# Low parts of the mixers' weights: an accumulating DMA in place of a subtraction

## The chip, the cores and the metric

The kernel runs on one core of one Trainium2 chip. The metric is the device time of one execution in microseconds (us). Five engines matter here: TensorE (PE in the profile; its weight loads are PEld) multiplies, VectorE (DVE), ScalarE (ACT) and GpSimd (POOL) do elementwise work, and SyncE (SP) issues most of the transfers. Each engine works through its own instruction list in order and waits at an instruction until what that needs is there.

## What is computed

The reference is two layers over 512 positions of 1024 features, all in float32. Each layer has a mixer and a feed-forward part:

```
h = rms_norm(x, attn_norm[l])
q_a, k_c, ..., c_q, c_kv, k_r, u = split(h @ w_in[l])
o_a = nsa_attention(q_a, k_c, ...)            # 6 heads: compressed, selected and window branch
o_b = mla_attention(c_q, c_kv, k_r, ..., w_uq, w_uk, w_uv)   # 6 heads
o_c = s5_ssm(u, ..., w_glu, b_glu)            # state-space groups
mix = concatenate([rms_norm(o_a), rms_norm(o_b), rms_norm(o_c)])
x = x + mix @ w_out[l]
x = x + conv_ffn(rms_norm(x, ffn_norm[l]), ffn_w_up[l], ..., ffn_w_down[l])
```

After the second layer comes a last rms_norm.

## The kernel before

Activations are kept transposed: features on the 128 partitions, the 512 positions along the row, so x is eight tiles of 128x512. Float32 accuracy comes from splitting: an operand is held as a high part (rounded to the format that TensorE takes at full rate, fp32r) and a low part (the operand less its high part), and `mm3` (lines 239 to 242) makes each product with three matmuls: high by high (line 240), weight high by activation low (241), weight low by activation high (242).

Every weight comes through `wload` (lines 232 to 237). SyncE loads 128 x n raw floats from HBM into one of 3 buffers `raw` (line 234). `split` then has ScalarE copy them, rounding, into the high half of one of 4 buffers `wt` (line 226), and GpSimd or VectorE subtract the high half from raw into the low half (line 227). Both sets of buffers are rings: a raw buffer is free for the next load when the subtraction has read it, a wt buffer when the last matmul that uses it is done. Which engine subtracts is set by `eng` in CFG for the weights named there (G is GpSimd, V VectorE); a `wload` without a name uses VectorE.

A layer goes through these weights in turn: 32 tiles of `win` (the input projection, 128x512), then among the attention heads one `wuv` (128x384), six `wuq` (128x384), three `wuk` (128x128), one `wglu` (128x512), and `wout1` (lines 1102 to 1112: for each of eight output tiles one of 128x256 and one of 128x384), then eight of 128x384 in the loop of lines 1150 to 1158, here called the last weights of w_out, whose product is scaled (line 1156), added to x (line 1157) and split for the feed-forward part. That part loads 88 tiles of `wup` (GpSimd subtracts) and 48 tiles of `wdn` (VectorE) a layer.

At the start ScalarE and VectorE split x (lines 229, 230) and square it (lines 286, 288), GpSimd adds the squares (line 294), TensorE sums them over partitions (line 253), and VectorE makes the reciprocal root from that (lines 256 to 268). The products of win begin before that root is known; it scales their results when they are taken out (line 689).

The program is written as tasks in an order by hand (PLAN0, PLAN1). Then a scheduler puts each engine's instructions in order by its own model of their durations; a change of what an instruction costs in that model can move others on every engine.

Of the kernel before, what the change touches and what calls it, by code (L numbers as in the profile page):

```python
# [13 lines left out]
AF = mybir.ActivationFunctionType  # L14
OP = mybir.AluOpType
# [6 lines left out]
D = 1024  # L22
# [108 lines left out]
def _pre(names):  # L131
    return tuple((n, -1, None) for n in names.split())


# The order in which each layer's mixer is issued. An entry is (task, step of the head pipeline, instruction of the
# tensor engine that it stays behind as (stage, unit) or None); step -1 comes before the first head.
PLAN0 = _pre('vc kc q2 cmp0 q0 tab krg q1 rope cmp1 ks kw pa0 vs sp0 gates pa1 ca sp1 pa2 sp2 pa3 sp3 ') + (
# [11 lines left out]
    ("w0", 17, (3, 13)), ("w1", 18, (0, 15)), ("w2", 19, (1, 16)), ("w3", 19, (3, 15)), ("w4", 20, (3, 16)))  # L149
CFG = dict(plan=(PLAN0, PLAN1), F=dict(main=15, aux=10, side=12), R=dict(main=16, side=3, q=3, pr=2), nraw=3, nw=4, hp=50,  # L150
           order=(2, 1, 3, 0), rings=dict(), tabs=2, lead=(0, 0, 3, 4), units=('NNNNNNMMMMMM', 'NNNNNNMMMMMM'), rest=((-7, -1, -1, -5, -7, -1, -1, -1), (-1, -1, -3, -1, -1, -1, -1, -1)),
           eng=dict(wo="G", mix="G", klo="G", csub="G", gel="G", win="G", wup="G", wdn="V", wo2="V", q="G", xadd="V"))


@with_exitstack
def tile_trunk(ctx, tc, xT_in, pos, cst_in, small_in, win, wuq, wuk, wuv, wglu, wout, wup, wdn,
# [6 lines left out]
    pp = ctx.enter_context(tc.tile_pool(name="pp", bufs=1, space=PSUM))  # L163

    def eng(n):
        return dict(V=V, G=G)[cfg["eng"][n]]

    def mk(shape, name, dt=F32):
        return cp.tile(shape, dt, name=name)
# [62 lines left out]
    def wload(src, n, E=None, w=None):  # L232
        raw = nxt("raw", raws)[:, :n]
        SY.dma_start(raw, src)
        w = w or nxt("w", wts)
        split(raw, w[:, 0, :n], w[:, 1, :n], E=E)
        return w

    def mm3(p, w, o, x, start, stop, n=128):
# [415 lines left out]
    for l in range(L):  # L655
# [114 lines left out]
                split(p[r0:r0 + 64], KF[b][r0:r0 + 64, 0], KF[b][r0:r0 + 64, 1])  # L770

        def mla_v():
            uv = wload(wuv[l], 384)
            mv.extend(R.get() for _ in range(3))
            for i in range(4):
                p = ps("mm")
                a0, a1 = ckv[0][:, 0, i * 128:(i + 1) * 128], ckv[0][:, 1, i * 128:(i + 1) * 128]
                PE.matmul(p[:, :384], lhsT=a0, rhs=uv[:, 0, :384], start=True, stop=False)
                PE.matmul(p[:, :384], lhsT=a0, rhs=uv[:, 1, :384], start=False, stop=False)
                PE.matmul(p[:, :384], lhsT=a1, rhs=uv[:, 0, :384], start=False, stop=True)  # L780
                for m in range(3):
                    v = mvv(m)[:, i]
                    split(shp(p[:, m * 128:(m + 1) * 128], 2, 64), v[:, :, 0, :], v[:, :, 1, :])
# [104 lines left out]

        def glu():
            area("side")  # L890
            gw = wload(wglu[l], 512)
            hb = sml(2)
            V.tensor_scalar(hb, S(l, "bglu"), 0.5, None, op0=OP.mult)
            oc = []
            for m in range(2):
                p = ps("x")
                for k in range(2):
                    mm3(p, gw, k * 256 + m * 128, zps[k], k == 0, k == 1)
                t = F.get()
                A.activation(t, p, AF.Tanh, bias=hb[:, m:m + 1], scale=0.5)  # L900
                V.scalar_tensor_tensor(t, t, 1.0, zs[m], op0=OP.add, op1=OP.mult)
                oc.append(t)
            F.free(*zs)
            R.free(*zps)
            mixc.extend(oc)
            area("main")
# [18 lines left out]
        def mla_unit(m, b):  # L925
            st = {}

            def proj_q():
                if b == 0:
                    p = ps("kq")  # L930
                    mm3(p, wload(wuk[l, :, m * 128:(m + 1) * 128], 128), 0, ckv[0], True, True)
                    for x in range(2):
                        r0 = 64 * x
                        split(p[r0:r0 + 64], KF[x][r0:r0 + 64, 0], KF[x][r0:r0 + 64, 1])
                uq = wload(wuq[l, m, :, b * 384:(b + 1) * 384], 384)
                p = ps("kq")
                for k in range(3):
                    mm3(p, uq, k * 128, cq[k], k == 0, k == 2)
# [211 lines left out]
        for c in range(8):  # L1150
            w = wload(wout[l, c, :, wcol[late]:wcol[late] + 384], 384, eng("wo2"))
            p = ps("mm")
# [170 lines left out]
```

## Time and profile before

| what | value |
|---|---|
| time, median of 3 runs (lowest to highest) | 1371.96 us (1371.95 to 1377.19) |
| span of the profiled execution | 1372.3 us |
| PE busy | 1302.4 us, 95% |
| DVE busy | 856.5 us, 62% |
| POOL busy | 724.4 us, 53% |
| ACT busy | 638.8 us, 47% |
| moved by DMA | 140.14 MB, 102 GB/s |

The profile is of one execution. Its span of 1372.3 us runs from its first recorded event to its last; no other time of that execution is recorded, so the span stands for it, and it is 0.3 us above the median of the timed runs.

In the span the first layer's mixer runs to about 322 us, its last weights of w_out to 351 us, its feed-forward part to 715 us; the second mixer follows to 976 us, its last weights of w_out to 1009 us, its feed-forward part to 1343 us, and the final norm ends it. An engine's row in a timeline gives the start, the duration, the line and the tiles, and in brackets the idle time of the engine before it with what ended that. A matmul's recorded duration overlaps that of its neighbours, so a rate is taken from the number of matmuls in a stretch.

### The profile page before, as it was taken

What the parts mean: (1) busy time and instruction counts of PE and PEld (TensorE: products, weight loads), DVE (VectorE), ACT (ScalarE), POOL (GpSimd) and SP (SyncE); (2) the same over time, 40 slices, a digit from 0 to 9 for tenths busy, and PEclk for the clock granted to TensorE, in tenths of its full rate; (3) what the DMA queues carried; (4) which work ended last, traced back from release to release, by engine and by line L of the source; (5) the groups of instructions that cost most, each with busy time, mean ns of one, the idle gap of its engine ahead of it and who ended that gap; (6) DMA issues with size and microseconds to landing.
All of it is one profiled execution on the core that took longest, in us unless ns stands there. A gap on an engine that the chain in (4) does not pass through costs nothing.

```text
span 1372.3 us, 19205 instructions
## 1 busy us (share of the span) xinstructions
PE 1302.4 (95%) x6414; PEld 1079.2 (79%) x6414; DVE 856.5 (62%) x1733; ACT 638.8 (47%) x1322; POOL 724.4 (53%) x722
## 2 busy tenths in 40 slices
PE   7888989998998999999999999999999999999997
PEld 5676777786876888888888887877878888888886
DVE  6988889858695334643466488986764433442455
ACT  4334667754443233423443356886453323332344
POOL 7485546654759155545437665556376315612532
PEclk9989999999999999999999999999999999999998
DMA  6243622212333333443353433121223333333332
GB/s 224 83 131 99 182 85 66 68 62 64 98 99 113 111 95 100 117 124 95 112 173 112 149 124 106 59 60 43 83 85 106 95 100 99 94 92 106 95 94 83
DMA packets 91556, 140.14 MB, mean 102 GB/s; under 512 B 15553, under 2 KB 36545, under 8 KB 91457
## 3 DMA queue, kind: packets, MB, share of 16 engines
q1 hardware_dynamic: 90176, 134.72, 32.2%
q0 software_dynamic: 1280, 4.20, 1.0%
q8 instruction: 50, 0.82, 0.3%
q14 instruction: 50, 0.40, 0.1%
HBM read 125.01 MB, written 15.96 MB: 103 GB/s over the span
## 4 chain that ended last, share of the span: by engine, by line
PE 72%; DVE 19%; issue 3%; POOL 2%; ACT 2%; DMA 2%; SPq 0%; DVEq 0%; POOLq 0%; ACTq 0%
PE bank L240 21%; PE bank L241 20%; PE bank L242 20%; DVE r L227 3%; PE bank L519 2%; PE bank L548 2%; DVE f L520 2%; PE bank L544 2%; DVE r L230 1%; DVE f L304 1%; DVE f L1157 1%; PE bank L271 1%; PE bank L816 1%; PE bank L253 1%; POOL wt L227 1%
## 5 line engine op out<-in xcount | busy, mean ns | idle before, releaser
L240 PE MATMUL bank<-r,wt 128*128 128x512 f32 x1466 | 580.9, 397 | 15.2 <-ACT wt L226 7.3
L241 PE MATMUL bank<-r,wt 128*128 128x512 f32 x1466 | 577.0, 394 | 4.4 <-DVE r L230 3.6
L242 PE MATMUL bank<-r,wt 128*128 128x512 f32 x1466 | 573.4, 394 | 5.1 <-POOL wt L227 5.1
L227 POOL TENSOR_TENSOR wt<-raw,wt 128x512 fp32r<-128x512 f32 (+2 forms) x272 | 355.0, 1309 | 300.1 <-ACT wt L226 291.0
L226 ACT CAST wt<-raw 128x512 fp32r<-128x512 f32 (+2 forms) x398 | 231.0, 584 | 332.5 <-PE bank L241 189.6
L240 PEld LDWEIGHTS bank<-r,wt 128*128 128x128 f32 x1466 | 278.2, 190 | 77.2 <-ACT wt L226 8.9
L242 PEld LDWEIGHTS bank<-r,wt 128*128 128x128 f32 x1466 | 278.0, 190 | 66.1 <-POOL wt L227 8.5
L241 PEld LDWEIGHTS bank<-r,wt 128*128 128x128 f32 x1466 | 278.4, 190 | 62.8 <-DVE r L230 6.5
L227 DVE TENSOR_TENSOR wt<-raw,wt 128x512 fp32r<-128x512 f32 (+3 forms) x126 | 88.9, 709 | 51.7 <-ACT wt L226 51.3
L294 POOL TENSOR_TENSOR f<-f,f 128x512 f32<-128x512 f32 (+1 forms) x53 | 68.0, 1284 | 99.9 <-ACT f L286 98.4
L532 POOL TENSOR_SCALAR f<-f,sml 128x128 f32<-128x128 f32 (+3 forms) x144 | 79.3, 569 | 52.2 <-DVE sml L530 18.0
L227 DVE TENSOR_TENSOR r<-bank,r 128x256 fp32r<-128x256 f32 (+4 forms) x196 | 90.2, 476 | 24.2 <-ACT r L226 23.0
L1182 DVE TENSOR_TENSOR f<-bank,f 128x512 f32<-128x512 f32 x44 | 30.3, 690 | 112.6 <-PE bank L242 103.1
L1188 POOL TENSOR_TENSOR f<-f,f 128x512 f32<-128x512 f32 x44 | 58.0, 1320 | 74.6 <-ACT f L1187 74.6
L523 ACT ACTIVATE f<-f,sml 128x384 f32<-128x384 f32 (+3 forms) x144 | 80.6, 560 | 32.5 <-DVE sml L520 31.6
L226 ACT CAST r<-bank 128x256 fp32r<-128x256 f32 (+4 forms) x196 | 79.0, 417 | 31.8 <-PE bank L544 15.7
L548 PE MATMUL bank<-r,r 128*128 128x512 f32 (+3 forms) x288 | 82.1, 353 | 10.4 <-DVE r L227 7.5
L519 PE MATMUL bank<-r,r 128*128 128x128 f32 (+3 forms) x336 | 79.3, 339 | 9.8 <-DVE sml L520 9.5
L226 ACT CAST r<-f 128x512 fp32r<-128x512 f32 (+1 forms) x76 | 46.9, 620 | 80.5 <-DVE f L1189 65.7
L520 DVE CUSTOM_DVE_ANT_0 f<-bank,cst 128x384 f32<-128x384 f32 (+3 forms) x144 | 67.8, 481 | 12.7 <-PE bank L519 11.6
L1189 DVE TENSOR_TENSOR f<-bank,f 128x512 f32<-128x512 f32 x44 | 30.4, 690 | 72.7 <-POOL f L1188 68.9
L1217 DVE TENSOR_TENSOR f<-bank,f 128x512 f32<-128x512 f32 x48 | 32.7, 688 | 65.6 <-PE bank L242 65.5
(225 smaller groups left out, 1549.9 us busy)
## 6 DMA issues: line engine op xcount, KB each, us to landing
raw<-in_wup_dram SPq DMA_DIRECT2D x176, 256.0 KB
raw<-in_wdn_dram SPq DMA_DIRECT2D x72, 256.0 KB
raw<-in_win_dram SPq DMA_DIRECT2D x64, 256.0 KB
f<-pd SPq DMA_DIRECT2D x32, 256.0 KB
raw<-in_wout_dram SPq DMA_DIRECT2D x32, 192.0 KB
f<-in_xT_dram SPq DMA_DIRECT2D x16, 256.0 KB
f<-in_w_dram SPq DMA_DIRECT2D x16, 256.0 KB
pd<-f SPq DMA_DIRECT2D x16, 256.0 KB
```

Of the source, the lines that this page charges most:

```text
L226: A.copy(hi, src)
L227: (E or V).tensor_tensor(lo, src, f32(hi), op=OP.subtract)
L240: PE.matmul(p, lhsT=w[:, 0, o:o + n], rhs=x[:, 0], start=start, stop=False)
L241: PE.matmul(p, lhsT=w[:, 0, o:o + n], rhs=x[:, 1], start=False, stop=False)
L242: PE.matmul(p, lhsT=w[:, 1, o:o + n], rhs=x[:, 0], start=False, stop=stop)
L294: G.tensor_tensor(a, a, q, op=OP.add)
L519: PE.matmul(p[:, :w], lhsT=q[:, i * 128:w], rhs=k[:, :w], start=n == 0, stop=n == len(passes) - 1)
L520: V.tensor_tensor_reduce(out=sm[i], in0=p[:, :w], in1=C("mask")[:, 512 - w:], op0=OP.add, op1=OP.min, scale=1.0, scalar=3.0e38, accum_out= ...
L523: A.activation(sm[i], sm[i], AF.Exp, bias=mx[:, i:i + 1], scale=-1.0, accum_out=su[:, i:i + 1])
L532: G.tensor_scalar(sm[i], sm[i], rs[:, i:i + 1], 1.0, op0=OP.mult, op1=OP.mult)
L548: PE.matmul(o[:, j * 128:], lhsT=v[j], rhs=pr[:, x, :w], start=first and j == 0 and x == 0, stop=last and j == 3 and x == 1)
L1188: G.tensor_tensor(t, t, r_f, op=OP.mult)
```

## The change

A third way to make a low part, "D", is added to `wload`. ScalarE still copies raw into the high half. Then ScalarE writes the negated high half into the low half, and GpSimd issues a DMA that reads the same weights from HBM a second time and adds them to what stands in the low half. The weights named wo, win and wo2 in `eng` go this way, and so do wuv, wglu, wuk and wuq; wup (GpSimd) and wdn (VectorE) stay as they are.

```diff
-           eng=dict(wo="G", mix="G", klo="G", csub="G", gel="G", win="G", wup="G", wdn="V", wo2="V", q="G", xadd="V"))
+           eng=dict(wo="D", mix="G", klo="G", csub="G", gel="G", win="D", wup="G", wdn="V", wo2="D", q="G", xadd="V"))
...
-        return dict(V=V, G=G)[cfg["eng"][n]]
+        return dict(V=V, G=G, D="D")[cfg["eng"][n]]
...
-        split(raw, w[:, 0, :n], w[:, 1, :n], E=E)
+        if E == "D":
+            A.copy(w[:, 0, :n], raw)
+            A.activation(w[:, 1, :n], w[:, 0, :n], AF.Identity, scale=-1.0)
+            G.dma_start(w[:, 1, :n], src, accum_op=OP.add)
+        else:
+            split(raw, w[:, 0, :n], w[:, 1, :n], E=E)
...
-            uv = wload(wuv[l], 384)
+            uv = wload(wuv[l], 384, "D")
...
-            gw = wload(wglu[l], 512)
+            gw = wload(wglu[l], 512, "D")
...
-                    mm3(p, wload(wuk[l, :, m * 128:(m + 1) * 128], 128), 0, ckv[0], True, True)
+                    mm3(p, wload(wuk[l, :, m * 128:(m + 1) * 128], 128, "D"), 0, ckv[0], True, True)
...
-                uq = wload(wuq[l, m, :, b * 384:(b + 1) * 384], 384)
+                uq = wload(wuq[l, m, :, b * 384:(b + 1) * 384], 384, "D")
```

In the changed kernel a line past the edit has a number five higher (240 is 245, 253 is 258, 294 is 299, 1156 is 1161), and the DMA is line 239.

Over both layers 134 weights are made in the new way: 64 of 128x512 (win), 32 of wout1 (16 of 128x256, 16 of 128x384), 16 last weights of w_out (128x384), and 22 others. That is 96 subtractions less on GpSimd, 38 less on VectorE, 134 instructions more on ScalarE and 134 DMAs more issued by GpSimd. TensorE has the same matmuls, in another order.

GpSimd's list near the program's start, before the change (line 227 is the subtraction of a weight, 294 the adding of squares; f8 and f9 gather the squares, wt0 to wt3 are the weights' buffers):

```order
L227 TENSOR_TENSOR wt0_127<-raw0_124,wt0_127 128x512
L227 TENSOR_TENSOR wt1_128<-raw1_125,wt1_128 128x512
L294 TENSOR_TENSOR f8_71<-f8_71,f10_73 128x512
L294 TENSOR_TENSOR f9_72<-f9_72,f11_74 128x512
L227 TENSOR_TENSOR wt2_129<-raw2_126,wt2_129 128x512
L992 MEMSET f3_66 128x64 x2
L294 TENSOR_TENSOR f8_71<-f8_71,f12_75 128x512
L294 TENSOR_TENSOR f9_72<-f9_72,f13_76 128x512
L992 MEMSET f4_67 128x64 x2
L623 TENSOR_SCALAR smt_160<-smt_160 128x2 x2
L227 TENSOR_TENSOR wt3_130<-raw0_124,wt3_130 128x512
L294 TENSOR_TENSOR f8_71<-f8_71,f14_77 128x512
```

And the same place after it (line 239 is the accumulating DMA, 299 the adding of squares):

```order
L239 DMA wt0_127<-in_win_dram 128x512
L239 DMA wt1_128<-in_win_dram 128x512
L299 ISA
L299 TENSOR_TENSOR f9_72<-f9_72,f11_74 128x512
L299 TENSOR_TENSOR f8_71<-f8_71,f10_73 128x512
L997 MEMSET f3_66 128x64 x2
L299 TENSOR_TENSOR f9_72<-f9_72,f13_76 128x512
L299 TENSOR_TENSOR f8_71<-f8_71,f12_75 128x512
L997 MEMSET f4_67 128x64 x2
L239 DMA wt2_129<-in_win_dram 128x512
L299 TENSOR_TENSOR f9_72<-f9_72,f15_78 128x512
L628 TENSOR_SCALAR smt_160<-smt_160 128x2 x2
```

Where four subtractions stood among the additions there are now the DMAs, and the DMAs of the third and fourth weight stand later among them.

TensorE's list at the place where it sums the squares over partitions (line 253), before the change:

```order
L242 MATMUL bank1_152<-r6_106,wt3_130 128x512
L240 MATMUL bank1_152<-r7_107,wt3_130 128x512
L241 MATMUL bank1_152<-r7_107,wt3_130 128x512
L242 MATMUL bank1_152<-r7_107,wt3_130 128x512
L253 MATMUL bank4_155<-ones_162,f8_71 128x1 x4
L253 MATMUL bank4_155<-ones_162,f9_72 128x1 x4
L242 MATMUL bank2_153<-r0_100,wt0_127 128x512
```

And after it, where that sum is line 258:

```order
L245 MATMUL bank1_152<-r4_104,wt3_130 128x512
L246 MATMUL bank1_152<-r4_104,wt3_130 128x512
L245 MATMUL bank2_153<-r0_100,wt0_127 128x512
L246 MATMUL bank2_153<-r0_100,wt0_127 128x512
L258 MATMUL bank4_155<-ones_162,f8_71 128x1 x4
L258 MATMUL bank4_155<-ones_162,f9_72 128x1 x4
L247 MATMUL bank0_151<-r4_104,wt2_129 128x512
```

The sum stood behind the last product of the first four weights; now it stands some 20 rows earlier, among products of wt0 and wt3, and most products with wt2 and wt3 come behind it.

VectorE's list at the last weights of w_out of the first layer, before the change (1156 scales a product, 1157 adds it to x, 230 makes the low part of x for the feed-forward part, 227 subtracts for a weight):

```order
L1156 TENSOR_TENSOR f13_76<-bank1_152,f16_79 128x512
L230 SCALAR_TENSOR_TENSOR r13_113<-f35_98,smt_160,r13_113 128x512
L1157 TENSOR_TENSOR f27_90<-f27_90,f13_76 128x512
L230 SCALAR_TENSOR_TENSOR r3_103<-f25_88,smt_160,r3_103 128x512
L227 TENSOR_TENSOR wt1_128<-raw2_126,wt1_128 128x384
L1156 TENSOR_TENSOR f1_64<-bank0_151,f16_79 128x512
L227 TENSOR_TENSOR wt2_129<-raw0_124,wt2_129 128x384
L230 SCALAR_TENSOR_TENSOR r4_104<-f27_90,smt_160,r4_104 128x512
L1157 TENSOR_TENSOR f30_93<-f30_93,f1_64 128x512
```

And after it (1161 and 1162 are the former 1156 and 1157):

```order
L1161 TENSOR_TENSOR f13_76<-bank1_152,f16_79 128x512
L230 SCALAR_TENSOR_TENSOR r13_113<-f35_98,smt_160,r13_113 128x512
L1162 TENSOR_TENSOR f27_90<-f27_90,f13_76 128x512
L230 SCALAR_TENSOR_TENSOR r3_103<-f25_88,smt_160,r3_103 128x512
L1161 TENSOR_TENSOR f1_64<-bank0_151,f16_79 128x512
L1162 TENSOR_TENSOR f30_93<-f30_93,f1_64 128x512
L230 SCALAR_TENSOR_TENSOR r4_104<-f27_90,smt_160,r4_104 128x512
```

The weights' subtractions are gone from the list; the rest is the same work in nearly the same order.

## Rows read from the trace of the kernel before

**Rows 1.** page: busy times of the engines; shares of the chain that ended last

```profile
PE 1302.4 (95%) x6414; PEld 1079.2 (79%) x6414; DVE 856.5 (62%) x1733; ACT 638.8 (47%) x1322; POOL 724.4 (53%) x722
...
PE 72%; DVE 19%; issue 3%; POOL 2%; ACT 2%; DMA 2%; SPq 0%; DVEq 0%; POOLq 0%; ACTq 0%
```

**Rows 2.** windows: length, busy (instructions) PE, PEld, DVE, ACT, POOL; clock, DMA share, GB/s

```profile
0.00:50.00 50.00, 39.48 (x178) 31.34 (x179) 37.16 (x66) 21.04 (x35) 33.06 (x34) 0.97 0.52 174
...
50.00:100.00 50.00, 40.46 (x186) 33.66 (x185) 46.23 (x86) 18.81 (x33) 35.73 (x41) 0.90 0.41 123
...
200.00:250.00 50.00, 48.06 (x274) 40.21 (x274) 42.76 (x131) 40.41 (x107) 28.71 (x38) 0.97 0.23 71
...
1050.00:1100.00 50.00, 50.00 (x222) 41.42 (x221) 23.29 (x29) 18.19 (x30) 18.62 (x15) 1.00 0.33 93
```

**Rows 3.** TensorE's waits: waiter <- releaser, us in total, times, longest

```profile
PE bank L519 <- DVE sml L520: 9.5, 8, 3.1
...
PE bank L242 <- POOL wt L227: 5.1, 7, 2.3
...
PE bank L829 <- DVE f L828: 3.6, 1, 3.6
...
PE bank L240 <- DVE f L1156: 3.0, 2, 1.6
...
PE bank L816 <- DVE bd L834: 2.3, 1, 2.3
```

**Rows 4.** timeline, GpSimd: start, duration, work [wait before it]

```profile
21.49 2.99 POOL L294 TENSOR_TENSOR f<-f,f 128x512 f32<-128x512 f32 x2
```

**Rows 5.** busy time and DMA load, 4 to 20 us

```profile
4.00:20.00 16.00, 10.67 (x30) 7.14 (x31) 13.08 (x11) 10.59 (x19) 12.89 (x14) 0.97 0.97 341
```

**Rows 6.** timeline, VectorE, 27 to 39 us

```profile
27.72 0.16 DVE L256 TENSOR_SCALAR sml<-bank 128x4 f32<-128x4 f32 x1 [5.64 <-PE bank L253]
...
36.28 0.69 DVE L304 SCALAR_TENSOR_TENSOR f<-f,f 128x512 f32<-128x512 f32 x1
...
37.22 1.78 DVE L304 SCALAR_TENSOR_TENSOR f<-f,f 128x512 f32<-128x512 f32 x1
```

**Rows 7.** GpSimd's subtractions of line 227, 24 to 112 us

```profile
24.00:112.00 88.00, 34.96 (x25) 0.94 0.37 112
```

**Rows 8.** granted clock after two waits of TensorE

```profile
67.00:70.00 3.00, 2.92 (x8) 2.44 (x9) 2.94 (x5) 2.19 (x3) 1.91 (x1) 0.50 0.01 3
...
118.00:125.00 7.00, 6.00 (x15) 4.62 (x16) 5.95 (x18) 2.01 (x7) 2.21 (x2) 0.51 0.32 90
```

**Rows 9.** timeline, VectorE, the last weights of w_out, first layer

```profile
330.21 1.03 DVE L227 TENSOR_TENSOR wt<-raw,wt 128x384 fp32r<-128x384 f32 x1
```

**Rows 10.** groups of one form: busy time, mean ns

```profile
L1187 ACT ACTIVATE f<-f 128x512 f32<-128x512 f32 x44 | 27.8, 632 | 66.9 <-DVE f L1185 66.9
...
L227 POOL TENSOR_TENSOR wt<-raw,wt 128x512 fp32r<-128x512 f32 x240 | 326.3, 1364 | 275.8 <-ACT wt L226 270.9 <-PE bank L242 1.9 <-PE bank L241 1.4
...
L227 DVE TENSOR_TENSOR wt<-raw,wt 128x384 fp32r<-128x384 f32 x38 | 24.1, 633 | 7.4 <-ACT wt L226 7.4
...
L683 POOL DMA_DIRECT2D f<-ud x4 | 2.4, 601 | 0.4 <-DMA ud<-f 0.4
```

**Rows 11.** GpSimd's own DMAs: size, median us from issue to landing

```profile
ud<-f POOLq DMA_DIRECT2D x4, 256.0 KB, 4.1
...
f<-ud POOLq DMA_DIRECT2D x4, 256.0 KB, 3.4
```

**Rows 12.** timeline, first weight of the second layer: cast, first low part

```profile
715.01 0.61 ACT L226 CAST wt<-raw 128x512 fp32r<-128x512 f32 x1
...
717.69 0.50 PE L242 MATMUL bank<-r,wt 128*128 128x512 f32 x1
```

**Rows 13.** timeline, a weight of w_out: cast, first low part

```profile
306.04 0.51 ACT L226 CAST wt<-raw 128x384 fp32r<-128x384 f32 x1 [0.93 <-PE bank L241]
...
309.73 0.39 PE L242 MATMUL bank<-r,wt 128*128 128x512 f32 x1
```

## Prediction

> **What bounds the kernel now.** I read the page first, then windows of 50 us, then TensorE's waits, then the timeline where those waits are long. TensorE is busy 1302.4 of 1372.3 us, and the chain that ended last runs 72% on it and 19% on VectorE [rows 1]: some 70 us are all that better supply can win, beside what matmuls lose at half clock. The windows say where: in the feed-forward part TensorE is busy 50.00 of 50 us, but 39.48 and 40.46 in the first two windows, where VectorE works 46.23 of 50 and GpSimd 35.73 [rows 2]. The idle time is the mixers', in the first 100 us above all. The feed-forward's weights are not touched, so I expect nothing there.
>
> TensorE's waits name VectorE first: 9.5 us for scores, 3.6 and 2.3 for the compressed branch (lines 829 and 816), 3.0 for the sums into x (1156). GpSimd's weight subtraction itself stands there with only 5.1 us in seven waits [rows 3]. So taking the subtraction away wins little directly; what it can win is VectorE's time, which GpSimd stretches: the same instruction of line 304 takes 0.69 us alone and 1.78 us at 37.22, under a subtraction [rows 6].
>
> **The change, term by term.** Low part alone, GpSimd: a 128x512 subtraction takes 1.36 us (240 such rows), and issuing a DMA of the same 256 KB from GpSimd 0.60 [rows 10]. So GpSimd is relieved by about 0.76 us a weight. VectorE loses 38 subtractions of 0.63 us, 24 us in all [rows 10]. ScalarE gains 134 negations; the nearest row, a 128x512 activation in place, takes 0.63 us [rows 10]: some 80 us on an engine that is never more than 40.41 busy of 50 in the windows shown [rows 2].
>
> *Latency of a low part.* Before, it lands a subtraction (1.36 us) behind the cast. After: negation 0.63, then issue to landing of an accumulating DMA, which the trace does not have. GpSimd's plain DMAs of 256 KB into and out of SBUF land after 3.4 and 4.1 us [rows 11]. Below 3.4 nothing speaks for it; above, an accumulation that reads its target first as a pass of its own would be up to twice that, 6.8. I take 4.5, near the rows. So a low part comes about 5.1 us behind the cast instead of 1.4.
>
> *What hides it.* A full load of win feeds 12 matmuls, at 50.00 us for 222 matmuls [rows 2] 2.7 us of TensorE. With four buffers, three others cover 8.1 us while one is refilled; less cast and negation (1.25) that leaves 6.9 us for the landing, so 4.5 is hidden in the steady state. The last weights of w_out feed nine matmuls: 6.1 us of cover, less two passes of 0.5, leaves 5.1; hidden, barely. It is not hidden where a weight is needed soon after its cast. The second layer's first weight is cast until 715.62 and its low part used at 717.69 [rows 12]: 2.07 us there, 5.1 needed, 3.0 lost. A weight of w_out is cast until 306.55 and used at 309.73 [rows 13]: 3.18 there, 4.8 needed, 1.6 lost. Sum **+5** for the late low parts; 0 if the scheduler's new order moves these uses back, +15 if the landing takes 6.8 (2.3 more at each of some four such places).
>
> *The start.* The subtractions between the additions of squares go, four of them: 4 x 0.76 = 3.0 us of GpSimd. The last squares are added until 24.48 [rows 4], and VectorE then sits idle 5.64 us until 27.72 for the sum that TensorE makes of them [rows 6]. TensorE's new list has that sum some 20 rows earlier, so up to 3 us come off the time at which VectorE's long list begins; with TensorE's own rows ahead of the sum out of the way, 4. Against it: from 4 to 20 us the transfers already keep the DMA engines 0.97 busy at 341 GB/s [rows 5], and four more reads of 0.26 MB are 1.05 MB, 3.1 us more of queue ahead of x's last tiles; the low part of the first weight is also wanted four rows of TensorE behind its first use. Bounds -4 to +3; I take **-1**.
>
> *VectorE, 24 to 112 us.* GpSimd makes 25 subtractions of line 227 there, 34.96 us; three of them are of activations and stay [rows 7]. Each of the other 22 stretched VectorE by 0 to 1.09 us (row 37.22 less row 36.28 [rows 6]), 0 to 24 us. VectorE is the engine that TensorE waits for here. What can come back is those waits (3.6 + 2.3, and 3.1 as the longest for scores [rows 3]) and what follows them: after the wait of 3.6 the granted clock is 0.50 from 67 to 70 us, after that of 3.1 it is 0.51 from 118 to 125 [rows 8], that is 1.2 and not 2.4 GHz, so 1.5 and 3.4 us are lost. Together 13.9. The relief is of the size of the waits, but GpSimd still adds, multiplies and casts beside VectorE; I take two thirds, **-9** (0 to -14).
>
> *Last weights of w_out, both layers.* VectorE loses 16 of its 38 subtractions, 10 us, one of which took 1.03 us at 330.21 [rows 9]. TensorE waits there 3.0 us for line 1156 in two waits [rows 3]. The wait at the head of the stage depends on the reciprocal root as well, so I take **-2** (-4 to 0).
>
> *ScalarE.* With about eight loads in 200 to 250 us and 0.5 us each it is 44 instead of 40.41 busy of 50 [rows 2], and its exponentials stand behind the negations. The cover is TensorE's own work, 48.06 of 50; if it fails, a wait of a negation's length in a few heads: 0 to +3, I take **0**. In the ring, a negation waits for the last low-part matmul of the buffer's former use, one matmul later than the cast did.
>
> Sum: 5 - 1 - 9 - 2 + 0 = **-7**. The profiled span is 1372.3 us, 0.3 above the median of the runs, so 1372.0 - 7 = **1365 us**.
>
> **A rule that speaks against it.** GpSimd's four DMA issues of line 683 took 601 ns in the mean [rows 10], with no sign of a block. The Trainium skill, "SBUF — State Buffer", section "Who interferes with whom", says that a DMA issued by GpSimd can be starved while VectorE holds the port pair the two share, as copies, casts and tensor_scalar operations in their two-port modes do. By it each landing would stretch by some tenths of a microsecond while VectorE is as busy as at 50 to 100 us: the sum would stand near -5 instead of -7, by an estimate of 0.4 us at a handful of short places. Four rows decide little; no run here shows an accumulating DMA.
>
> **Rivals.**
>
> *The landing is slow (slower).* If an accumulating DMA lands only after 8 us, the ring of four no longer hides it. Place: the projections and the last weights of w_out. Price: at win 8 - 6.9 = 1.1 us a turn, a quarter per load, 64 loads: 18, of which other work of TensorE hides half, 9; at the last weights of w_out (8 - 5.1)/4 x 16 = 12; the four short places 3.5 us worse each, 14 on top of the 5. Less the relief of 12: 9 + 12 + 19 - 12 = +28, **1400 us**. At 6.5 us it is 0 + 6 + 13 - 12 = +7, from where it decides. For it: nothing in the trace accumulates, and the early DMA engines are full [rows 5]. Against: 3.4 and 4.1 us for the plain ones [rows 11], and a DMA share of 0.23 to 0.41 after the first 50 us [rows 2].
>
> *The relief is eaten (no change).* The chain through VectorE from the start to 112 us keeps its length because x comes 3 us later and GpSimd's remaining work stretches VectorE as before: -9 becomes -3, the start +1, w_out -1, late parts +5: +2, **1374 us**. For it: 19% of the chain on VectorE is mostly its own work.
>
> *More comes back.* The first two windows hold 20 us of idle TensorE [rows 2]. If VectorE is early enough from 28 us on, all of its 13.9 us go, the start gives 4, w_out 4, and the low parts cost 2: -20, **1352 us**.
>
> **Chances.** The forecast 0.42, spread from 1357 to 1373; the slow landing 0.20, from 1378 to 1410; the relief eaten 0.20, from 1368 to 1380; more comes back 0.18, from 1343 to 1357. The range that leaves no more than 2 in 10 out is **1347 to 1390**; the forecast's own is 1357 to 1373. A difference under 0.5%, 6.9 us, is about what a measurement here can't tell from none. Faster by more, under 1365.1: all of the last case and 0.26 of the forecast's 0.42, 0.44. Slower by more, over 1378.8: the slow landing and little of the eaten relief, 0.23. Within: the rest, 0.33.
>
> **What would show it.** Right: in the changed profile VectorE's rows of line 304 near 37 us are 0.7 us and not 1.78; VectorE's idle time before the reciprocal root ends by 25 us; the waits of 3.6 and 3.1 us and the half clock behind them shrink; new waits of TensorE name the weight's DMA, in total some 5 us, the largest near the second layer's first weight; the landing stands at 4 to 5 us. Wrong: landings of 6.5 us and more with waits of the low-part matmul spread over the projections; a start in which x arrives later than 20 us and nothing is won by 112; a feed-forward part that changes its length; or waits for ScalarE among the heads of several microseconds.

## The result and the profile after

The changed kernel takes 1394.95 us (median of 4 runs, 1393.77 to 1404.0), the kernel before beside it 1374.58 us (1371.95 to 1377.43). The ratio is 1.0159, with a 95% interval from 1.0123 to 1.0196: about 20 us slower, where 1365 us, 7 us faster, was forecast, and outside the range that ended at 1390. The profiled execution has a span of 1392.0 us, 19.7 us more than before.

The page of the changed kernel, its busy times, its DMA queues and its chain [rows 1]:

```profile
PE 1305.2 (94%) x6414; PEld 1081.1 (78%) x6414; DVE 813.8 (58%) x1695; ACT 703.9 (51%) x1456; POOL 711.1 (51%) x760
...
q1 hardware_dynamic: 90176, 134.72, 32.5%
q0 software_dynamic: 20576, 33.04, 14.3%
...
PE 67%; DVE 10%; DMA 5%; POOL 5%; issue 4%; ACT 3%; SPq 0%; DVEq 0%; POOLq 0%; ACTq 0%
```

VectorE has become 43 us lighter, as meant, and its share of the chain has fallen from 19% to 10%; but DMA stands there with 5% in place of 2%, and POOL too. TensorE's own work is the same, so the 20 us are idle time and time at half clock. GpSimd has lost only 13 us: the issues eat most of what the subtractions gave back.

TensorE's waits after [rows 3] (waiter, releaser, us in total, times, longest):

```profile
PE bank L247 <- DMA wt<-in_win_dram: 18.8, 11, 6.5
PE bank L553 <- DVE r L227: 11.2, 16, 1.5
PE bank L245 <- ACT wt L237: 8.4, 3, 6.0
PE bank L245 <- DVE f L1161: 8.4, 3, 3.8
```

The waits for VectorE at lines 829 and 816 that headed the forecast (3.6 and 2.3) are gone from the list. In their place are the low parts' DMA, and the sums into x (line 1161, the former 1156), which went from 3.0 to 8.4 us.

Where the difference arises is read by setting the two timelines beside each other at landmarks that both kernels have: VectorE's first instruction of a reciprocal root (line 256, later 261), and the last time that it takes a product of win out in the first layer (line 689, later 694). "d" is the start in a kernel less the start before, in us, from the profiled execution of each. Behind "after" the columns are the runs e1, e2, e5, e3, e8, e9, e11 and e15 of the next section. A column is one execution, and not always a typical one: that of e1 took 2.9 us and that of e11 5.0 us more than its run's median, those of e5, e8 and e15 some 2 us less.

| landmark (us before) | after | win only | w_out only | last of w_out only | small only | no DMA, negated only | negated, then added | after + wup by VectorE | same, quarter |
|---|---|---|---|---|---|---|---|---|---|
| first root, 27.7 | -3.0 | -1.8 | 0.0 | +0.3 | -0.6 | -0.7 | +0.9 | -1.7 | -3.5 |
| last of win, 169.3 | -6.4 | -4.0 | +0.3 | -0.1 | +2.6 | -20.2 | +6.0 | -4.7 | -12.2 |
| ahead of the last of w_out, 318.4 | +3.8 | +1.9 | -0.6 | -2.3 | +6.1 | -9.5 | +9.1 | +5.4 | -7.1 |
| behind it, 352.7 | +8.7 | +3.4 | +4.5 | +2.5 | +6.1 | -11.4 | +8.3 | +3.7 | -8.8 |
| second layer's first root, 725.9 | +15.0 | +9.2 | +7.2 | +6.1 | +6.2 | -11.5 | +11.1 | +9.9 | -5.8 |
| ahead of its last of w_out, 973.6 | +14.7 | +9.7 | +7.1 | +5.1 | +5.1 | -9.5 | +14.8 | +10.0 | -6.6 |
| behind it, 1009.6 | +19.7 | +9.7 | +10.4 | +10.3 | +5.1 | -8.9 | +16.8 | +11.3 | -6.4 |
| last root, 1362.7 | +19.9 | +9.6 | +10.7 | +10.4 | +6.6 | -8.7 | +17.0 | +11.5 | -6.2 |

The other columns belong to the experiments. The column "after" alone says: the first projections do win (3.0 us at the first root, 6.4 at the last of win), then the heads of the first layer lose 10.2, the last weights of w_out 4.9 and 5.0, and the second layer's start about 5. In the projections and heads of the second layer, some 250 us, nothing changes.

**The start and the landing.** The first root, and the wait for the first low part, in the changed kernel's timelines [rows 6]:

```profile
24.71 0.16 DVE L261 TENSOR_SCALAR sml<-bank 128x4 f32<-128x4 f32 x1 [2.58 <-PE bank L258]
```

```profile
14.56 0.80 PE L247 MATMUL bank<-r,wt 128*128 128x512 f32 x1 [6.52 <-DMA wt<-in_win_dram]
```

The root comes 3.0 us earlier although TensorE stands for 6.52 us on its first low part. The windows from 4 to 20 us [rows 5] and over the half clock among the heads:

```profile
4.00:20.00 16.00, 7.53 (x18) 5.36 (x19) 13.02 (x11) 12.72 (x23) 11.50 (x15) 1.00 1.01 335
172.00:190.00 18.00, 17.01 (x72) 15.75 (x73) 8.99 (x31) 6.62 (x16) 8.90 (x13) 0.53 0.46 131
```

The DMA engines are full (1.01), and the landings up to 24 us are slow, 5.3 to 8.3 us. The second row is a stretch in which the heads lose: TensorE is busy 17.01 of 18 us, at a granted clock of 0.53, the lower of its two levels (1.2 GHz) almost throughout. Landings of the accumulating DMAs (size, median us from issue) [rows 11], and what issuing them costs GpSimd (busy, mean ns, idle before) [rows 10]:

```profile
wt<-in_win_dram POOLq DMA_DIRECT2D x64, 256.0 KB, 5.4
...
wt<-in_wout_dram POOLq DMA_DIRECT2D x32, 192.0 KB, 3.9
```

```profile
L239 POOL DMA_DIRECT2D wt<-in_win_dram x64 | 57.0, 922 | 56.7 <-ACT wt L238 53.4 <-ACT r L226 1.2 <-ACT f L514 1.0
```

So 5.4 us and not 4.5, and 0.92 us for an issue and not 0.60 (as recorded; at 334.66 and 1004.85 GpSimd's next instruction begins 0.61 us after the issue's start). The ring hides 5.4 as worked out: from 740 to 840 us, where the landings have a median of 5.1, TensorE waits 0.2 us for them.

**The second layer's start.** Its third cast in the kernel before, and the changed kernel's timeline [rows 12]:

```profile
718.26 0.60 ACT L226 CAST wt<-raw 128x512 fp32r<-128x512 f32 x1
```

```profile
724.97 0.60 ACT L237 CAST wt<-raw 128x512 fp32r<-128x512 f32 x1
...
728.59 0.60 ACT L237 CAST wt<-raw 128x512 fp32r<-128x512 f32 x1
...
729.24 0.50 PE L245 MATMUL bank<-r,wt 128*128 128x512 f32 x1 [1.60 <-ACT wt L237]
...
731.11 0.50 PE L247 MATMUL bank<-r,wt 128*128 128x512 f32 x1 [1.14 <-DMA wt<-in_win_dram]
```

TensorE waits 1.60 us for a cast, and then low parts land late (1.14, later 0.67 and 0.36 us). The first weight is cast at 724.97, 10.0 us later than before, as TensorE's work is there; the cast that TensorE waits for is the third, 10.3 us later than before. So the negations hold this cast up by only 0.3 us; most of the 1.60 us is that TensorE, whose new list puts low parts later, comes to the third weight before it is cast.

**The last weights of w_out.** Three timelines of the changed kernel, VectorE, GpSimd and TensorE, from 332 to 341 us [rows 9]:

```profile
333.91 1.41 DVE L1162 TENSOR_TENSOR f<-f,f 128x512 f32<-128x512 f32 x1
335.24 4.66 DVE L230 SCALAR_TENSOR_TENSOR r<-f,smt,r 128x512 fp32r<-128x512 f32 x1
339.82 0.68 DVE L1161 TENSOR_TENSOR f<-bank,f 128x512 f32<-128x512 f32 x1
```

```profile
332.57 0.87 POOL L239 DMA_DIRECT2D wt<-in_wout_dram  x1 [1.11 <-ACT wt L238]
333.43 1.33 POOL L299 TENSOR_TENSOR f<-f,f 128x512 f32<-128x512 f32 x1
334.66 0.93 POOL L239 DMA_DIRECT2D wt<-in_wout_dram  x1
335.27 1.65 POOL L227 TENSOR_TENSOR wt<-raw,wt 128x512 fp32r<-128x512 f32 x1
336.52 1.61 POOL L299 TENSOR_TENSOR f<-f,f 128x512 f32<-128x512 f32 x1
337.74 1.60 POOL L227 TENSOR_TENSOR wt<-raw,wt 128x512 fp32r<-128x512 f32 x1
```

```profile
340.56 0.80 PE L245 MATMUL bank<-r,wt 128*128 128x512 f32 x1 [3.78 <-DVE f L1161]
```

This was in no step of the forecast. GpSimd's list now has DMAs whose negation is not there yet (1.11 us at 332.57); behind them its other work, the first wup weights' subtractions and the squares (line 299), runs without a gap from 335.27 to 339.34. VectorE's instruction of line 230, 0.74 us when alone, begins beside the first of the three and ends behind the last, 4.66 us. TensorE waits 3.78 us for the sum behind it, and 340 to 344 us are partly at half clock (0.57). At 1005 us the same happens, again 4.66 us.

The wait at the DMA and the series without a gap do not explain the row by themselves. In the kernel before, GpSimd and VectorE in the same stage:

```profile
334.35 1.30 POOL L294 TENSOR_TENSOR f<-f,f 128x512 f32<-128x512 f32 x1 [1.96 <-ACT f L286]
335.61 1.75 POOL L227 TENSOR_TENSOR wt<-raw,wt 128x512 fp32r<-128x512 f32 x1
337.31 3.44 POOL L294 TENSOR_TENSOR f<-f,f 128x512 f32<-128x512 f32 x2
340.72 3.41 POOL L227 TENSOR_TENSOR wt<-raw,wt 128x512 fp32r<-128x512 f32 x2
```

```profile
334.67 3.24 DVE L1157 TENSOR_TENSOR f<-f,f 128x512 f32<-128x512 f32 x2
337.83 3.47 DVE L230 SCALAR_TENSOR_TENSOR r<-f,smt,r 128x512 fp32r<-128x512 f32 x2
```

Six instructions follow each other there, and VectorE takes its turn between them: none of its instructions takes longer than 1.78 us. And ahead of the row at 1005.37 GpSimd was not held at a DMA:

```profile
1003.62 1.28 POOL L299 TENSOR_TENSOR f<-f,f 128x512 f32<-128x512 f32 x1 [0.55 <-ACT f L291]
1004.85 0.86 POOL L239 DMA_DIRECT2D wt<-in_wout_dram  x1
1005.46 1.58 POOL L227 TENSOR_TENSOR wt<-raw,wt 128x512 fp32r<-128x512 f32 x1
```

What both rows of 4.66 us have in common is the issue of an accumulating DMA 0.5 to 0.6 us ahead. In the kept traces every VectorE instruction of 128x512 above 2.4 us has such an issue less than 2 us ahead of it, and the kernels without these DMAs (before, e8, e9, e13, e16) have no such instruction; but one of 64x512 takes 3.78 us in the kernel before, at 128.50, so the issue is not the only way to it. What makes VectorE lose its turn stays open.

### The profile page after: what moved, and what is told of

Same layout as the page of the kernel before. It is cut to its first block, busy times and chain, and to the rows that moved or that the text cites. A ratio compares the mean times of both kernels' runs of the same rounds, so it can differ in the third digit from the quotient of the medians.

```text
span 1392.0 us, 19420 instructions
## 1 busy us (share of the span) xinstructions
PE 1305.2 (94%) x6414; PEld 1081.1 (78%) x6414; DVE 813.8 (58%) x1695; ACT 703.9 (51%) x1456; POOL 711.1 (51%) x760
## 3 DMA queue, kind: packets, MB, share of 16 engines
q1 hardware_dynamic: 90176, 134.72, 32.5%
q0 software_dynamic: 20576, 33.04, 14.3%
## 4 chain that ended last, share of the span: by engine, by line
PE 67%; DVE 10%; DMA 5%; POOL 5%; issue 4%; ACT 3%; SPq 0%; DVEq 0%; POOLq 0%; ACTq 0%
PE bank L247 19%; PE bank L245 19%; PE bank L246 19%; PE bank L553 2%; PE bank L524 2%; DMA wt<-in_win_dram 2%; PE bank L549 2%; DVE r L227 2%; DVE r L230 1%; DVE f L525 1%; DMA wt<-in_wout_dram 1%; PE bank L276 1%; POOL wt L227 1%; PE bank L258 1%; POOL f L537 1%
## 5 line engine op out<-in xcount | busy, mean ns | idle before, releaser
L227 POOL TENSOR_TENSOR wt<-raw,wt 128x512 fp32r<-128x512 f32 x176 | 235.2, 1339 | 248.5 <-ACT wt L226 245.0
L226 ACT CAST wt<-raw 128x512 fp32r<-128x512 f32 (+2 forms) x264 | 159.0, 606 | 240.6 <-PE bank L246 137.8
L237 ACT CAST wt<-raw 128x512 fp32r<-128x512 f32 (+3 forms) x134 | 72.4, 541 | 86.2 <-PE bank L246 62.5
L1187 DVE TENSOR_TENSOR f<-bank,f 128x512 f32<-128x512 f32 x44 | 30.1, 689 | 114.6 <-PE bank L247 103.7
L227 DVE TENSOR_TENSOR wt<-raw,wt 128x512 fp32r<-128x512 f32 (+2 forms) x88 | 66.5, 762 | 45.9 <-ACT wt L226 45.8
L528 ACT ACTIVATE f<-f,sml 128x512 f32<-128x512 f32 (+3 forms) x144 | 80.6, 561 | 17.6 <-DVE sml L525 14.5
L239 POOL DMA_DIRECT2D wt<-in_win_dram x64 | 57.0, 922 | 56.7 <-ACT wt L238 53.4
L525 DVE CUSTOM_DVE_ANT_0 f<-bank,cst 128x512 f32<-128x512 f32 (+3 forms) x144 | 67.7, 482 | 13.8 <-PE bank L524 12.5
```

The costliest lines, as they stand in the source:

```text
L226: A.copy(hi, src)
L227: (E or V).tensor_tensor(lo, src, f32(hi), op=OP.subtract)
L237: A.copy(w[:, 0, :n], raw)
L525: V.tensor_tensor_reduce(out=sm[i], in0=p[:, :w], in1=C("mask")[:, 512 - w:], op0=OP.add, op1=OP.min, scale=1.0, scalar=3.0e38, accum_out= ...
L528: A.activation(sm[i], sm[i], AF.Exp, bias=mx[:, i:i + 1], scale=-1.0, accum_out=su[:, i:i + 1])
```

## The experiments

Theory A: low parts land late, and TensorE waits for them. Theory B, formed on the row of 4.66 us: GpSimd's list, held at a DMA, bunches its other work, which locks VectorE out. Rivals: C, the load on ScalarE and the DMA engines anywhere; D, the scheduler's changed order by itself. Times are medians; ratios are to the kernel before, run beside it, with their 95% intervals.

**The parts alone.**

```diff
# e1_win:  eng wo="G", win="D", wo2="V"; the four small loads without "D"
# e2_wout: eng wo="D", win="G", wo2="D"; the four small loads without "D"
# e3_small: eng wo="G", win="G", wo2="V"; the four small loads with "D"
```

> Only the 64 loads of win (input projection) by the accumulating DMA; w_out, wuv, wglu, wuk, wuq as before. Theory A (low parts land too late, 4.5 to 10 us, and TensorE waits for them, at the starts of the layers above all): most of the loss stays, since 18.8 of the 21 us of waits for the DMA are for win: 1383 to 1390. Theory B (the loss is made at the last weights of w_out, where GpSimd's list waits for a negation and then runs three instructions back to back that lock VectorE out for 4.7 us): that stage is as before, the 10 us of it are gone, 1378 to 1384 with the 5 us at the second layer's start kept. Rival C (more time on ScalarE and on the DMA engines everywhere): 1380, half of the loss, in proportion to the loads.

> Only the 48 loads of w_out (wout1 and the last weights) by the accumulating DMA; win and the rest as before. Theory A: 2.1 us of waits for these DMAs, so 1374 to 1377. Theory B: both stages of the last weights lose 4 to 5 us each, with a VectorE instruction of line 230 stretched to over 4 us under back-to-back GpSimd work: 1380 to 1384. Rival C: 1378 to 1380.

> Only the 22 loads of wuv, wglu, wuk, wuq by the accumulating DMA. Theories A and B both: within 3 us of before, 1370 to 1376, the one waits 0.2 us for these in the changed kernel, the other has no bunching there. Rival C: 1375. If it is 1380 or more, the half-clock stretch from 172 to 190 us of the changed kernel comes from these loads (they lie there).

Measured: win 1380.83 us (1.0064, 1.0045 to 1.0082), w_out 1384.63 (1.0092, 1.0077 to 1.0107), small 1380.61 (1.0058, 1.0042 to 1.0075). w_out is the largest, as B has it (0.6 us above its range): its first stage has the same VectorE row, at 330.79. Win is faster than A's range and inside B's, and 1380 is also what C gave; of its loss, 5.8 us lie between 352.7 and 725.9, at the second layer's start (table), which is A's place. The small weights' 8 us were foreseen by none of the theories. The three sum to 28 and not 20.

**The first weights of each layer left to GpSimd** (e4, on the changed kernel; the edit shortened).

```diff
-        return wload(win[l, ...], 512, eng("win"))
+        seen.append(l); return wload(win[l, ...], 512, G if seen.count(l) <= 4 else eng("win"))
```

> The changed kernel, but the first four weights of each layer's win have their low part made by GpSimd's subtraction. Theory A: the first wait of 6.5 us and the waits at 729 to 738 us (3.8 us) go: 1392 less 5 at the second layer's start and less 0 to 6 at the first: 1381 to 1387. Theory B: only the second layer's start gains, 1387 to 1390, and the 10 us at the last weights of w_out stay. Rival C: 1391.

Measured: 1395.3 us (1.0171, 1.0151 to 1.0192), no gain, and above the range of every theory. The 6.52 us go, and the last of win comes 10.9 us earlier than in the kernel before, but at 318.4 us nothing of that is left (-0.1). In the second layer the start loses 0.6 us and not 5.2, but the wait moves: at 744.74 us TensorE waits 1.40 us for a weight that now comes by the DMA, and the granted clock is 0.50 from 747 to 748 us. In this layer the price sits at the change from ready weights to landing ones, wherever that is put.

**The last weights of w_out alone, and wup's first weights taken from GpSimd.**

```diff
# e5_wo2: eng wo="G", win="G", wo2="D"; the four small loads without "D"
# e11_wupV, on the changed kernel:
-                    w = wload(wup[l, m, ...], 512, eng("wup"))
+                    w = wload(wup[l, m, ...], 512, V if m == 0 else eng("wup"))
```

> Only the 16 last weights of w_out (128x384) by the accumulating DMA; all else as before. The runs of parts gave +8 for win, +12 for w_out, +8 for the small ones, each alone. Theory B (GpSimd's list, held at the DMA's wait for a negation, then runs a weight subtraction of the feed-forward and additions of squares back to back and locks VectorE out): this part carries most of the 12: 1380 to 1384, with VectorE's line 230 at over 4 us near 335 and 1000 us. Rival D (any change of the scheduler's order costs some 6 to 10 us, wherever it is made): 1378 to 1382, without such a row. If the loss is wout1's: 1372 to 1375.

> The changed kernel, but the first four weights of wup of each layer have their low part made by VectorE and not by GpSimd, so that GpSimd has only additions of squares and DMAs in its list at the last weights of w_out. Theory B: the instruction of line 230 of 4.66 us goes back under 2 us and the waits of 3.8 and 3.3 us for line 1161 shrink: 6 us faster than the changed kernel, 1385 to 1390. Theory A: unchanged, 1392 to 1397. Rival D: anything from 1388 to 1398.

Measured: the 16 loads alone, 1386.63 us (1.0107, 1.009 to 1.0123), all of w_out's loss; with wup's first weights on VectorE, 1380.56 (1.0062, 1.0038 to 1.0086), where the changed kernel had 1.0159; that is more than twice the 6 us that B gave. The VectorE row of the first, and the same instruction's longest in the stage of the second:

```profile
329.08 4.67 DVE L230 SCALAR_TENSOR_TENSOR r<-f,smt,r 128x512 fp32r<-128x512 f32 x1
```

```profile
331.63 1.85 DVE L230 SCALAR_TENSOR_TENSOR r<-f,smt,r 128x512 fp32r<-128x512 f32 x1
```

The row comes with these 16 loads in both layers and goes with GpSimd's subtractions among them; the stages then cost -1.7 and +1.3 us instead of 4.9 and 5.0. Part of that is no cure of the DMA: the same move in the kernel before (e13, below) makes the two stages 3.0 us shorter and 0.4 us longer. With wup's first weights on VectorE in both, the DMAs cost the stages 1.4 and 0.9 us. So it is shown that these 16 DMAs, with GpSimd's subtractions among them, make the rows and the loss of some 10 us; the half of B that has GpSimd's wait at the DMA as the reason is not shown (the series ahead of 1005.37 has no such wait). VectorE's group of line 230, in the changed kernel and in this one:

```profile
L230 DVE SCALAR_TENSOR_TENSOR r<-f,smt,r 128x512 fp32r<-128x512 f32 x44 | 58.1, 1324 | 22.1 <-ACT r L229 21.8
```

```profile
L230 DVE SCALAR_TENSOR_TENSOR r<-f,smt,r 128x512 fp32r<-128x512 f32 x44 | 50.6, 1154 | 22.5 <-ACT r L229 22.3
```

**No DMA: negated only; negated and then added by an engine.**

```diff
# e8_none
-            G.dma_start(w[:, 1, :n], src, accum_op=OP.add)
# e9_neg: GpSimd for win and wout1, VectorE for the others
+            E.tensor_tensor(w[:, 1, :n], raw, f32(w[:, 1, :n]), op=OP.add)
```

> The changed kernel without the DMA: the low part stays the negated high part (the addition of the raw weight is left out). ScalarE's negations stay, GpSimd and VectorE have neither subtraction nor DMA for these weights. Theory A (the landing is late) and theory B (GpSimd waits, then bunches): no wait for a landing and none on GpSimd, so all of the 20 us go and the relief shows: 1355 to 1368. Rival C (ScalarE's negations cost): stays above 1378. Rival D (the order): 1372 to 1385, with waits of TensorE for VectorE among the heads.

> Negations on ScalarE as in the changed kernel, but then GpSimd (win, wout1) or VectorE (the others) adds raw to the negated high part, in place of the DMA. No accumulating DMA, no landing, the elementwise work of before, 80 us more of ScalarE. Theories A and B: near before, 1372 to 1378. Rival C: 1380 to 1390, the negations alone make the loss. Rival D: 1378 to 1385.

Measured: 1367.3 us (0.996, 0.9945 to 0.9975) and 1390.02 (1.0127, 1.0112 to 1.0142). The first, which leaves the addition out, bounds the relief for its order of the lists: with no subtraction and no DMA at all, ScalarE's negations kept, the gain is 5.5 us. So the DMAs, with the order that goes with them, cost some 27 us of the changed kernel (0.996 to 1.0159), and the negations are not what makes the loss when nothing follows them. The second contradicts A and B, and lies at the upper end of what C gave (1390): the work of before, put one ScalarE instruction later, loses 17 us. Its longest waits stand early:

```profile
PE bank L247 <- POOL wt L239: 6.3, 3, 4.2
PE bank L834 <- DVE f L833: 6.1, 1, 6.1
...
PE bank L245 <- DVE gates L757: 4.3, 1, 4.3
```

It fits that a low part that comes later costs here, by whatever means, but this run does not tell that from its changed order: C in the sense of "ScalarE is too busy" is ruled out by the first run, D is not.

**A quarter of the columns** (e15). On the kernel with wup's first weights on VectorE; the addition to the other columns is left out:

```diff
-            G.dma_start(w[:, 1, :n], src, accum_op=OP.add)
+            G.dma_start(w[:, 1, :128], src[:, :128], accum_op=OP.add)
```

> As the changed kernel with the first four wup weights by VectorE (1380.6), but each accumulating DMA adds only the first 128 columns of the weight (the addition to the other columns is left out), so that it lands after some 3 us and reads a quarter to a half of the bytes, with the same instructions and waits. Theory A (the landing makes what is left of the loss): TensorE's waits for these DMAs fall from 20 us to under 10, and the time to 1370 to 1375. Rival D (the order): 1378 to 1382, as without.

Measured: 1370.2 us (0.9978, 0.9965 to 0.9991), 10 us less than with the full width. Landings and waits:

```profile
wt<-in_win_dram POOLq DMA_DIRECT2D x64, 64.0 KB, 3.4
```

```profile
PE bank L247 <- DMA wt<-in_win_dram: 9.3, 4, 5.3
```

With the same instructions and issues, a landing after 3.4 us and a fourth of the bytes remove what was left of the loss: the waits for win's DMA go from 17.8 to 9.3 us, and from 352.7 to 725.9 us, where the second layer's start lies, 3.0 us are lost and not 6.2 (table). This is A, as far as the bytes are not told from the landing; the two profiled executions lie 17.7 us apart and the medians 10, so the stages are compared with that reserve. The time is also that of e13 (0.997), which has no DMA and no negation: with a quick landing, the issues, the negations and the changed order together cost about what the saved subtractions bring.

**Each DMA in two halves** (e18). Also on the kernel with wup's first weights on VectorE (1380.56):

```diff
-            G.dma_start(w[:, 1, :n], src, accum_op=OP.add)
+            [G.dma_start(w[:, 1, a:b], src[:, a:b], accum_op=OP.add) for a, b in ((0, n // 2), (n // 2, n))]
```

> The changed kernel with the first four wup weights by VectorE (1380.6), each accumulating DMA cut into two over half the columns each, so that the products with the first half wait only for the first. The same bytes, twice the issues on GpSimd. Theory A with the landing as the cause: waits for these DMAs fall from 20 to some 12 us, 1374 to 1379. If the bytes on the DMA engines are the cause: no gain, 1380 to 1385, and GpSimd's 0.87 us more per weight may add to it.

Measured: 1420.03 us (1.0344, 1.0313 to 1.0375). Landings, and GpSimd's issues:

```profile
wt<-in_win_dram POOLq DMA_DIRECT2D x128, 128.0 KB, 5.2
```

```profile
L239 POOL DMA_DIRECT2D wt<-in_win_dram x128 | 122.0, 1319 | 47.8 <-ACT wt L238 45.9 <-ACT f L514 1.4 <-issue 0.5
```

A half lands no earlier than a whole (5.2 against 5.3 us), and each issue takes 1.32 us instead of 0.92, so GpSimd's issues for win take twice as long for the same bytes and the loss grows by 40 us. TensorE's waits for win's DMA did fall from 17.8 to 9.4 us, as A had it, and yet no theory had such a time. The run does not separate landing from bytes, which it was meant to; it shows that twice the issues cost far more than the shorter waits bring, and not where.

**The order.** GpSimd in place of VectorE for the small weights, and wuk alone taken back:

```diff
# e16_smallG: wuv, wglu, wuk, wuq by GpSimd's subtraction, all else as before
# e17_wukV: wuv, wglu, wuq by the DMA, wuk by VectorE, all else as before
```

> The kernel before, but the 22 weights wuv, wglu, wuk, wuq have their low part made by GpSimd's subtraction and not VectorE's; no DMA. It changes TensorE's order in about as many rows (356 lines of difference) as the same weights by DMA did (429). Rival D (a changed order among the heads costs by itself): 1377 to 1384, like the run with only the small weights by DMA, 1380.6. Theory A: 1370 to 1375.

> Of the small weights wuv, wglu and wuq by the accumulating DMA, wuk (six of 128x128) back on VectorE; all else as before. With all four by DMA it was 1380.6 (8 us over), TensorE waiting 2.2 us for wuk's DMA. Theory A (a landing near its use): most of the 8 us go, 1372 to 1376. Rival D (the changed order, or the negations among the heads): still 1378 to 1382.

Measured: 1375.96 us (1.0016, 1.0004 to 1.0029) and 1380.8 (1.0051, 1.0034 to 1.0068). A changed order with the old method costs about 2 us here, less than D gave; wuk's short slack is not the cause of the 8. Among the small ones the waits for the DMA are 2.2 us or none, and the loss lies among the heads (+6.1 at 318.4). What makes it stays open.

**Combinations.**

```diff
# e13_before_wupV: the kernel before, wup's first four weights a layer by VectorE
# e14_mix: the DMA for win of the first layer from its fifth weight and for w_out; wup as in e13
# e19_wupV_smallV: the DMA for win and w_out; wup as in e13
```

> The kernel before, but the first four weights of wup of each layer have their low part made by VectorE and not by GpSimd; no accumulating DMA anywhere. Theory B: if GpSimd's subtractions of these weights also lock VectorE out in the kernel before (rows of line 230 of 1.78 us near 331 us and 3.5 us for two near 338), it gains 2 to 5 us: 1368 to 1371. If the lockout needs the DMA's wait in GpSimd's list: no change, 1371 to 1375.

> The accumulating DMA for win of the first layer only, from its fifth weight on, and for w_out of both layers; win of the second layer, wuv, wglu, wuk, wuq as before; the first four weights of wup by VectorE. Theory A and B together (what costs is a layer's start, the small weights, and the lockout): 1366 to 1374, the relief without its price. Rival D (order, wherever changed): 1376 to 1384.

> The accumulating DMA for win and w_out only, wuv, wglu, wuk and wuq as before, the first four wup weights by VectorE. If the parts add up: 1380.6 less the 8 us of the small weights, 1371 to 1375, which leaves win's late landings (8 us) against the relief. Rival D: 1377 to 1383.

Measured: 1370.75 us (0.997, 0.996 to 0.998), 1378.01 (1.0032, 1.0017 to 1.0046) and 1385.49 (1.009, 1.0068 to 1.0112). The first, with no DMA in it, is the only one of all the runs that leaves no addition out and beats the kernel before: the contention was in that too, smaller, with VectorE's line 230 at 1.78 us under the subtraction. The third such instruction of the stage in the kernel before and in e13:

```profile
331.16 1.78 DVE L230 SCALAR_TENSOR_TENSOR r<-f,smt,r 128x512 fp32r<-128x512 f32 x1
```

```profile
328.26 0.74 DVE L230 SCALAR_TENSOR_TENSOR r<-f,smt,r 128x512 fp32r<-128x512 f32 x1
```

The mix gave no gain and lies in D's range: the DMA in the cheapest places still costs 7 us against e13. And e19, at 1.0090, is no faster than e11 at 1.0062 (the intervals overlap), though it has 22 DMAs fewer, and lies above both forecasts: the parts do not add up, by up to the size of the small weights' loss.

## Why the prediction was wrong

The forecast was -7: start -1, VectorE -9, late parts +5, last weights of w_out -2, ScalarE 0. Two of its steps failed.

- **Last weights of w_out: a step that failed, -2 forecast, +9.9 measured** (4.9 and 5.0). VectorE does lose its subtractions there, but the step took GpSimd's DMA as work that frees GpSimd. It is an instruction that waits for ScalarE in GpSimd's list (90.3 us in 52 waits, over the whole kernel), and behind its issue, in each layer once, VectorE stands still for 4.66 us over three two-input instructions; TensorE's wait for the sums grew from 3.0 to 8.4 us. The forecast had only the pairwise stretch (0.69 to 1.78 us). Why the rows come is open; that they come with these 16 DMAs beside GpSimd's subtractions is shown. The Trainium skill, "SBUF — State Buffer", section "Who interferes with whom", says that a VectorE instruction with two SBUF inputs contends with a GpSimd instruction that reads SBUF; the trace agrees (0.74 us alone, 1.78 us beside one subtraction), and has two rows that last over three of them.
- **VectorE, -9 to 112 us: the other step that failed, and the larger miss.** Start and VectorE together were to be some 10 us ahead, and at 318.4 us the kernel is 3.8 us behind. The relief itself came: line 304 is back at 0.69 us, the waits of 3.6 and 2.3 us are gone, and the last of win comes 6.4 us earlier, 20.2 without the DMA. What failed is that the step let an early arrival count to the end. All of it, and more, is lost again by 318.4 us: after +10.2, win only +5.9, quarter +5.1; without the DMA 10.7 of the 20.2. The kernels that do not arrive early at 169.3 (w_out only, last of w_out only) lose nothing there (-0.9, -2.2). The upper bound of the whole relief is therefore 5.5 us (e8), where the forecast put 12. That the heads have a bound of their own which gives back any early arrival fits these columns, but the runs that arrive late lose there as well (small +3.5, negated then added +3.1), so it is argued, not shown, and the cause stays open. The small weights' DMAs are not needed for it: e19, without them, loses 10.7 us there, and e14 14.1. Nor is the half clock from 172 to 190 us: the granted clock of e19 is 1.00 in that stretch.
- **Late parts, +5:** at the second layer's start 5.2 us, where 3.0 was worked out; the term left out that TensorE's new order would meet the third weight before its cast (1.60 us). The loss comes with win's DMAs there: 5.9 us in e1 and 5.7 in e19, 0.6 or less in e2, e3, e5, e4 and e14, whose first weights of that layer are subtracted as before. The landing was 5.4 us, taken as 4.5. In the steady state it is hidden, as worked out. The weight of w_out at 306 us had its wait (1.11 us at 314 us, forecast 1.6).
- **Start, -1:** -3.0 at the first root, within its bounds, for the reason given (the last squares are added until 20.90 us and not 24.48), in spite of 6.5 us on the first low part.
- **The rival of a slow landing** had nearly the right sum (1400) for a reason that is only half right: 5.4 us are under the 6.5 from which it was to decide, and half of the loss is not the landing. What failed in the range is that no rival had GpSimd's list, or the heads, as its place.

Tallied against 19.9: last weights of w_out 9.9 (shown by e5 and e11 to come with its 16 DMAs), the second layer's start 5.2 (win's DMAs there; A, by e15 with the reserve on bytes), heads of the first layer 10.2 (open), less 6.4 for the projections; the rest, +1.0, lies in the first feed-forward part.

## What to carry to other kernels

An instruction that is cheap on its engine can be dear for its neighbours: look at what runs just behind it in that engine's list, and at which other engine works beside that. A DMA in place of an elementwise instruction trades a short busy time for a landing of several microseconds, so count, for each place of use, the time between the input's being ready and its use; where a ring refills it is hidden, at the start of a stage it is not. And a gain in one stage is worth only what the next stages let through: in the kernel without the DMA, 20 us at 169 us were 9 at the end.

## What the runs showed of the hardware

- An accumulating DMA takes about twice the DMA engines' time of a plain one. GpSimd's queue went from 4.20 MB in 1.0% of the 16 engines' span to 33.04 MB in 14.3%: 0.46% per added MB, against 32.5% for 134.72 MB, 0.24%, on the plain queue.
- A VectorE instruction with two SBUF inputs, 0.74 us alone, stood for 4.65 to 4.67 us over three GpSimd instructions without a gap, in four kernels (the changed one, e2, e4, e5), each time 0.5 to 0.6 us behind the issue of an accumulating DMA. A series without a gap alone does not do it: beside six in a row in the kernel before, VectorE's longest took 1.78 us.
- The issue of an accumulating DMA of 128 rows is recorded on GpSimd with 0.92 us for 2 KB rows, and with 1.32 us for 1 KB rows issued in pairs; a plain one with 0.60.
- An accumulating DMA from HBM landed 5.4 us (median) after its issue for 256 KB, 3.9 for 192 KB and 3.4 for 64 KB (e15); a half of 128 KB issued in a pair took 5.2 (e18).
